# A new order of loads and of work in the opening of a transformer-like kernel, and its first constants on another queue

## The chip, the cores and the metric

One Trainium2 chip, of which one core is used. The metric is the device time of one execution in microseconds (us). The kernel before takes 1350.43 us (median of three runs, 1349.74 to 1351.45).

The core's engines run in parallel, each with its own list of instructions in order: TensorE (PE, with its weight loads as PEld), VectorE (DVE), ScalarE (ACT), GpSimd (POOL) and SyncE (SP), which here only issues loads. They wait for each other by semaphores.

## The reference

Two layers over 256 latent tokens and 256 context tokens of width 1024, in float32. The first layer mixes tokens by an mLSTM, the second by multi-head latent attention; each is followed by a gated convolutional feed-forward network. What the opening computes is the start of the first layer, for the latent tokens x with condition c and for the context with condition c_ctx:

```python
def _modulation(cond, w, b):
    m = jax.nn.silu(cond) @ w + b              # w: 1024 x 6144
    return jnp.split(m[:, None, :], 6, axis=-1)

def _modulate(x, shift, scale):
    return x * (1 + scale) + shift
...
ml = _modulation(c, ada_w[i], ada_b[i])
mc = _modulation(c_ctx[None, :], ada_w[i], ada_b[i])
hl = _modulate(x, ml[0], ml[1])
hc = _modulate(xc, mc[0], mc[1])
...
x_m = h @ w_up                                 # 1024 x 2048, inside the mLSTM mixer
```

So: two products of a single row with a matrix (shift and scale), an elementwise step, and a matrix product.

## The kernel before, in words

A float32 product is made of three products of numbers split in a high and a low part (hi, lo): hi times hi, hi times lo, lo times hi. The split is a cast by ScalarE and a subtraction by VectorE. Weights come in a stream of pieces of 128 x 1024 numbers through a class `Stream`; each piece is loaded by SyncE into one of a few buffers, split into one of three `w` buffers and used.

The opening (`start_up`) works on eight tiles f = 0 to 7, each 128 of the 1024 input channels, and multiplies them with the first six column blocks (`NUP`) of w_up. For each tile it loads from memory:

- `adaw`: the modulation's weights. For f under 4 (`NFD`) two pieces with shift and scale, 512 KB each; for f from 4 on one piece with the shift alone.
- `adat`, for f from 4 on: the scale's weights transposed, 512 KB; the scale is then not made on TensorE but by sums on VectorE.
- `xT`: the tile's tokens transposed, 256 KB.
- `raw`: the tile's rows of w_up, 384 KB.

Beside these come a few constants (`sm`, whose first 32 columns hold the conditions, and the rest, 211 KB) and the two conditions spread over all partitions (`bc`, 512 KB each).

The work on a tile is cut into steps with names, and a list, `PLAN` (lines 53 to 61), gives the order in which they are written out. Within the opening TensorE, VectorE, ScalarE and SyncE keep that order (`manual_schedule`), each for its own instructions; beyond it a planner orders most of the work by its estimates and priorities. The steps for tile f:

- `Zn`: n matmuls of zeros, 512 columns each, ahead of all else (TensorE, L710).
- `rowsf0`, `rowsf1`: condition times `adaw`, on column groups of the array (TensorE, L548). For f from 4 on there is only `rowsf0`.
- `copyf`: the result out of PSUM (VectorE for f = 0, else ScalarE, L555).
- `Tf`: small matmuls that turn the rows into columns (TensorE, L560).
- `colsf`: bias added (VectorE, L567).
- `sumf0`, `sumf1`, f from 4 on: the scale of either condition, a product with `bc` summed up (VectorE, L576). `siluj` prepares `bc` (ScalarE, L744).
- `hf0`, `hf1`: the modulation of either half of the tokens, into the high part (L664 on VectorE or L666 on ScalarE); `xxf0`, `xxf1`: the same in full precision; `hlof`: the low part (VectorE, L741).
- `whif`, `wlof`: high and low part of the tile's w_up rows (ScalarE L715, VectorE L720). There are three `w` buffers, so `whi` of tile f waits until the ups of tile f - 3 are done.
- `upf0`, `upf1`, `upf2`: hi times hi, hi times lo, lo times hi, six matmuls of 512 columns each, one per column block, added up in six PSUM banks over all tiles (TensorE, L732).

Loads are issued by SyncE in program order (`load(f)`, L684): tiles 0 to 3, then `bc`, then tile 4; the loads of tiles 5 to 7 are written behind `wlo0` to `wlo2`, since their w_up rows go into buffers that these free. Tiles 3 and 4 borrow two other buffers for them. Behind the opening `w_up` goes on with ten more column blocks from the stream (L462 to L464, three matmuls for each of eight tiles), evacuates the six held banks, and computes the later modulations on VectorE beside them (L597). The main program calls `setup`, `start_up` and `w_up` in turn.

Of the kernel before, what the change touches and what calls it, by code (L numbers as in the profile page):

```python
# [7 lines left out]
F32 = mybir.dt.float32  # L8
# [9 lines left out]
T = SEQ + CTX  # L18
# [13 lines left out]
NB, NRAW, NU, NS = 3, 3, 31, 15  # L32
# [18 lines left out]
NUP = 6  # L51
NFD = 4
PLAN = """
Z7 rows00 rows01 whi0 copy0 T0 rows10 cols0 h00 h01 wlo0 xx00 xx01 up00 hlo0 rows11 up02 copy1 whi1 T1 up01
cols1 h10 h11 xx10 xx11 wlo1 hlo1 rows20 up10 rows21 up12 copy2 whi2 T2 up11 cols2 h20 h21 xx20 xx21 wlo2 hlo2 silu0
rows30 up20 rows31 up22 copy3 whi3 T3 up21 cols3 h30 h31 xx30 xx31 wlo3 hlo3 silu1
rows40 up30 copy4 sum40 T4 up32 whi4 sum41 cols4 up31 h40 h41 xx40 xx41 wlo4 hlo4
rows50 up40 copy5 sum50 T5 up42 whi5 sum51 cols5 up41 h50 h51 xx50 xx51 wlo5 hlo5
rows60 up50 copy6 sum60 T6 up52 whi6 sum61 cols6 up51 h60 h61 xx60 xx61 wlo6 hlo6
rows70 up60 copy7 sum70 T7 up62 whi7 sum71 cols7 up61 h70 h71 xx70 xx71 wlo7 hlo7 up70 up72 up71  # L60
""".split()
# [372 lines left out]
class K:  # L434
# [63 lines left out]
    def setup(self):  # L498
        nc, p = self.nc, self.pool
        a = self.a  # L500
        self.sm = p.tile([128, a["sm"].shape[1]], F32, name="sm")
        nc.sync.dma_start(self.sm[:, :32], a["sm"][:, :32])
        b1 = self.smc("ada_b")[:, 8:16]
# [13 lines left out]
        nc.vector.memset(self.zero.bitcast(F32), 0.0)  # L517
        self.condp = p.tile([128, 8, 32], F32, tag="s2", name="condp", bufs=NS)
        nc.vector.memset(self.condp, 0.0)
# [153 lines left out]
    def start_up(self):  # L673

        nc, st = self.nc, self.st
        self.hT = []
        self.xcd = self.dr.tile([16, 128, 512], F32, name="xcd")
        self.xmd = self.dr.tile([16, 128, 512], F32, name="xmd")
        self.t2d = {(p, j): self.dr.tile([128, 1024], F32, name="t2d") for p in range(2) for j in range(4)}
        self.xA, self.x1, self.xc, self.xcr = {}, {}, [], []  # L680
        w, raws = [], []
        self.adaw, self.adap, self.adar, self.adat, self.xT = {}, {}, {}, {}, []

        def load(f):  # L684
            if f < NFD:
                for h in range(2):
                    t = self.uf("adaw")
                    nc.sync.dma_start(t, self.a["adaf"][f, h])
                    self.adaw[f, h] = t
            else:  # L690
                self.adaw[f, 0] = t = self.uf("adaw")
                nc.sync.dma_start(t, self.a["adas"][f])
                self.adat[f] = t = self.uf("adat")
                nc.sync.dma_start(t, self.a["adaT"][0, 1, f])
            for op in ("w", "x") if f == 0 else ("x", "w"):
                if op == "x":
                    x = self.s2("xT")
                    nc.sync.dma_start(x, self.a["tokT"][f])
                    self.xT.append(x)
                    continue  # L700
                tag, bufs = ("ar", 2) if f in (3, 4) else ("raw", NRAW)
                r = self.pool.tile([128, 1024], F32, tag=tag, name="raw0", bufs=bufs)
                nc.sync.dma_start(r[:, :NUP * 128], st.ws[st.ids["upf", f, 0][0], :, :NUP * 128])
                raws.append(r)
            if f == 2:
                nc.sync.dma_start(self.sm[:, 32:], self.a["sm"][:, 32:])

        def warm(n):
            for _ in range(n):
                nc.tensor.matmul(ps[-1], self.zero[:, 0:128], self.zero, start=True, stop=True)  # L710

        def w_hi(f):
            t = self.pool.tile([128, 2, CW], F32R, tag="w", name="w", bufs=NB)
            n = NUP * 128
            nc.scalar.copy(t[:, 0, :n], raws[f][:, :n])  # L715
            w.append(t)

        def w_lo(f):
            t, n = w[f], NUP * 128
            nc.vector.tensor_sub(t[:, 1, :n], raws[f][:, :n], t[:, 0, :n])  # L720
            if f < 3:
                load(f + 5)

        ps = [self.ps("up") for _ in range(NUP)]
# [10 lines left out]
        def h(f, g):  # L735
            if len(self.hT) == f:
                self.hT.append(self.u("hT"))
            self.mod_part(f, g, self.hT[f][:, 0])
# [4 lines left out]
        def silu(j):  # L743
            nc.scalar.activation(self.bc[j], self.bc[j], AF.Silu)  # L744

        ops = {"Z": warm, "rows": self.ada_rows, "copy": self.ada_copy, "T": self.ada_T, "cols": self.ada_cols,
               "sum": self.ada_sum, "silu": silu, "whi": w_hi, "wlo": w_lo,
               "h": h, "xx": lambda f, g: self.mod_part(f, g, self.xT[f]), "hlo": hlo, "up": up}
        e = mybir.EngineType
        with self.tc.manual_schedule(engines={e.PE, e.DVE, e.Activation, e.SP}):  # L750
            for f in range(4):
                load(f)
            self.bc_load(False)
            load(4)
            for t in PLAN:
                name = t.rstrip("0123456789")
                ops[name](*map(int, t[len(name):]))
            st.pump(10)
        self.ps_up = ps

    def conv(self, ps, w3, b, tmp, n):
# [1512 lines left out]
```

## Time and profile before

| | |
|---|---|
| median of three runs | 1350.43 us |
| profiled execution | 1350.77 us, of which the span of the instructions is 1348.7 us |
| TensorE busy | 1335.7 us, 99% of the span |
| VectorE, ScalarE, GpSimd busy | 1072.6, 708.2, 123.1 us |
| granted TensorE clock, mean | 0.997 |
| DMA | 292.09 MB, mean 217 GB/s |
| first matmul of the weight stream behind the opening | 56.16 us (its weight load) |

The profile gives the busy time of each engine, the chain of work that ended last, the instructions in order of time with what ended the idle time before them ("<-"), and busy times by stretch. A busy TensorE may still run below its pace, since matmuls overlap and the clock varies; the granted clock is given as a share of full speed.

### The profile page before, as it was taken

The numbers are of one execution on the slowest core, as the hardware profiler recorded it, in microseconds if no ns is written. First come the engines' busy times: TensorE is split into PE (matmuls) and PEld (weight loads), VectorE is DVE, ScalarE is ACT, GpSimd is POOL, SyncE is SP. The second block draws the span as 40 slices with busy tenths as digits, with TensorE's granted clock in tenths as the row PEclk, the third lists the DMA queues.
The fourth block names the chain that finished last, engine by engine and source line by source line (L and its number), as shares of the span: only waits on it lengthen the run. The fifth ranks groups of instructions, "written<-read, shape, count | busy, mean of one in ns | idle before, by whom it ended". The sixth has DMA issues, their size and how long they took to land.

```text
span 1348.7 us, 18734 instructions
## 1 busy us (share of the span) xinstructions
PE 1335.7 (99%) x6661; PEld 1120.0 (83%) x6661; DVE 1072.6 (80%) x1774; ACT 708.2 (53%) x1239; POOL 123.1 (9%) x216
## 2 busy tenths in 40 slices
PE   8999999999999999999999999999999999999997
PEld 5777888888888888888898888888888998988886
DVE  4798757587888696777889887778887798898884
ACT  3675434435644545374644333343458757677661
POOL 0032000011011010120002000000100011000100
PEclk8999999999999999999999999999999999999999
DMA  9689748879766364756737777775877424476860
GB/s 368 250 297 347 251 155 249 251 262 316 264 199 207 111 233 131 239 195 216 237 127 245 224 243 238 239 235 164 242 259 245 137 72 157 159 214 197 267 188 32
DMA packets 88093, 292.09 MB, mean 217 GB/s; under 512 B 11640, under 2 KB 12152, under 8 KB 88000
## 3 DMA queue, kind: packets, MB, share of 16 engines
q1 hardware_dynamic: 61840, 215.77, 48.8%
q0 software_dynamic: 17520, 57.70, 14.0%
q10 hardware_dynamic: 8640, 17.44, 3.5%
q8 instruction: 52, 0.85, 0.3%
q14 instruction: 41, 0.34, 0.1%
HBM read 260.28 MB, written 30.58 MB: 216 GB/s over the span
## 4 chain that ended last, share of the span: by engine, by line
PE 95%; DMA 2%; DVE 1%; ACT 1%; SPq 0%; issue 0%; DVEq 0%; ACTq 0%
PE fin L1589 8%; PE y L1673 7%; PE fin L462 6%; PE fin L464 6%; PE tok L462 6%; PE fin L463 6%; PE tok L463 6%; PE tok L464 6%; PE qk L462 4%; PE qk L464 4%; PE qk L463 4%; PE y L463 4%; PE y L462 4%; PE y L464 4%; PE up L462 1%; PE up L464 1%
## 5 line engine op out<-in xcount | busy, mean ns | idle before, releaser
L378 DVE TENSOR_TENSOR w<-raw,w 128x1024 fp32r<-128x1024 f32 (+1 forms) x256 | 307.8, 1206 | 112.5 <-ACT w L375 111.8
L375 ACT CAST w<-raw 128x1024 fp32r<-128x1024 f32 (+1 forms) x256 | 265.2, 1038 | 240.7 <-PE tok L464 84.4
L597 DVE SCALAR_TENSOR_TENSOR junk<-ar,bc 128x1024 f32<-128x1024 f32 x128 | 155.9, 1218 | 3.2 <-ACT mod L612 2.0
L463 PE MATMUL fin<-h,w 128*128 128x512 f32 (+1 forms) x376 | 141.2, 376 | 0.0
L462 PE MATMUL fin<-h,w 128*128 128x512 f32 (+1 forms) x376 | 141.2, 376 | 0.0
L464 PE MATMUL fin<-h,w 128*128 128x512 f32 (+1 forms) x376 | 141.1, 375 | 0.0
L1589 PE MATMUL fin<-h,w 128*128 128x256 f32 (+1 forms) x624 | 108.7, 337 | 0.0
L1589 PEld LDWEIGHTS fin<-h,w 128*128 128x128 f32 x624 | 95.9, 190 | 12.5
L462 PE MATMUL qk<-xc,w 128*128 128x512 f32 x256 | 100.4, 392 | 0.0
L464 PE MATMUL qk<-xc,w 128*128 128x512 f32 x256 | 99.7, 390 | 0.0
L463 PE MATMUL qk<-xc,w 128*128 128x512 f32 x256 | 99.6, 389 | 0.0
L463 PEld LDWEIGHTS fin<-h,w 128*128 128x128 f32 x376 | 70.8, 188 | 12.9
L464 PEld LDWEIGHTS fin<-h,w 128*128 128x128 f32 x376 | 70.8, 188 | 12.9
L462 PEld LDWEIGHTS fin<-h,w 128*128 128x128 f32 x376 | 70.7, 188 | 12.8
L464 PEld LDWEIGHTS qk<-xc,w 128*128 128x128 f32 x256 | 48.1, 188 | 10.1
L463 PEld LDWEIGHTS qk<-xc,w 128*128 128x128 f32 x256 | 48.1, 188 | 9.7
L462 PEld LDWEIGHTS qk<-xc,w 128*128 128x128 f32 x256 | 48.1, 188 | 9.7
L771 ACT ACTIVATE fg<-fg 128x512 f32<-128x512 f32 (+1 forms) x44 | 23.1, 526 | 57.3 <-DVE fg L769 51.0
L462 PE MATMUL tok<-w,hT 128*128 128x512 f32 x128 | 49.9, 390 | 0.0
L464 PE MATMUL tok<-w,hT 128*128 128x512 f32 x128 | 49.8, 389 | 0.0
L463 PE MATMUL tok<-w,hT 128*128 128x512 f32 x128 | 49.8, 389 | 0.0
L1673 PE MATMUL y<-w,fz 128*128 128x512 f32 x198 | 46.7, 393 | 0.3 <-DVE w L378 0.2
(489 smaller groups left out, 3141.2 us busy)
## 6 DMA issues: line engine op xcount, KB each, us to landing
raw<-in_ws SPq DMA_DIRECT2D x281, 512.0 KB, 4.7
ar<-in_adaT SPq DMA_DIRECT2D x80, 512.0 KB, 4.9
raw<-in_ws POOLq DMA_DIRECT2D x13, 512.0 KB, 7.2
raw<-in_ws SPq DMA_DIRECT2D x12, 384.0 KB, 6.0
adaw<-in_adaf SPq DMA_DIRECT2D x8, 512.0 KB, 6.5
xmd<-xr POOLq DMA_DIRECT2D x16, 256.0 KB, 4.8
xcd<-cv POOLq DMA_DIRECT2D x16, 256.0 KB, 4.9
xs<-xmd POOLq DMA_DIRECT2D x16, 256.0 KB, 5.5
```

What stands on the lines that cost most here:

```text
L375: k.nc.scalar.copy(h[:, :cols], src)
L378: k.nc.vector.tensor_sub(l[:, :cols], src, h[:, :cols])
L462: mm(out, w[0], x[0], start=start, stop=False)
L463: mm(out, w[0], x[1], start=False, stop=False)
L464: mm(out, w[1], x[0], start=False, stop=stop)
L597: nc.vector.scalar_tensor_tensor(o, w, 1.0, self.bc[j], op0=ALU.mult, op1=ALU.mult, accum_out=col[:, k, j:j + 1])
L771: nc.scalar.activation(tmp[:, :n], tmp[:, :n], AF.Silu)
L1589: nc.tensor.matmul(ps[:, :m], w[x][:, k * 128:(k + 1) * 128], hT(k)[:, :m], start=k == 0 and x == j, stop=k == 7 and x != j, skip_group_ch ...
L1673: nc.tensor.matmul(ps[b], a[:, p, ts], w[q][:, cs], start=j == 0 and n == 0 and not more, stop=j == end and n == 2, skip_group_check=True)
```

## The change

Five things change.

1. The order of the steps (`PLAN`) is another one. up00 stands ahead of rows10; rows of two or three tiles stand together; the sums of a tile come earlier against its h; the last four steps remain up61, up70, up72, up71.
2. New steps `Yn`: n matmuls of zeros with 256 columns, one behind rows00, two behind rows01, four behind T0.
3. The loads have a list of their own, `LOADS`, cut where a load of w_up rows would need a buffer that is not free yet. In it a40 comes ahead of a31, w3 and x3, the `bc` loads come behind x3, and t4, a50 and later loads are mixed anew. The bytes are the same.
4. The first 32 columns of `sm` are loaded by ScalarE's queue instead of SyncE's.
5. `condp`, the padded condition, lives in a buffer of the large ring (31 buffers) instead of the small one (15).

Lists become dictionaries where tiles are now touched out of order. The diff, with its last part cut to what matters:

```diff
@@ -51,13 +51,15 @@
 NUP = 6
 NFD = 4
 PLAN = """
-Z7 rows00 rows01 whi0 copy0 T0 rows10 cols0 h00 h01 wlo0 xx00 xx01 up00 hlo0 rows11 up02 copy1 whi1 T1 up01
-cols1 h10 h11 xx10 xx11 wlo1 hlo1 rows20 up10 rows21 up12 copy2 whi2 T2 up11 cols2 h20 h21 xx20 xx21 wlo2 hlo2 silu0
-rows30 up20 rows31 up22 copy3 whi3 T3 up21 cols3 h30 h31 xx30 xx31 wlo3 hlo3 silu1
-rows40 up30 copy4 sum40 T4 up32 whi4 sum41 cols4 up31 h40 h41 xx40 xx41 wlo4 hlo4
-rows50 up40 copy5 sum50 T5 up42 whi5 sum51 cols5 up41 h50 h51 xx50 xx51 wlo5 hlo5
-rows60 up50 copy6 sum60 T6 up52 whi6 sum61 cols6 up51 h60 h61 xx60 xx61 wlo6 hlo6
-rows70 up60 copy7 sum70 T7 up62 whi7 sum71 cols7 up61 h70 h71 xx70 xx71 wlo7 hlo7 up70 up72 up71
+Z7 rows00 Y1 rows01 whi0 copy0 Y2 T0 cols0 h00 h01 wlo0 xx00 xx01 Y4 hlo0 up00 rows10 rows11 up02 copy1 T1 up01 whi1
+rows20 wlo1 cols1 h10 rows21 xx10 h11 up12 xx11 hlo1 copy2 up11 whi2 up10 T2 cols2 rows30 h21 xx21 rows31 rows40 copy3
+h20 xx20 wlo2 up20 hlo2 T3 cols3 h30 copy4 whi3 h31 T4 xx30 xx31 wlo3 hlo3 silu0 silu1 whi4 up21 sum40 up22 sum41 up30
+cols4 up31 wlo4 h41 h40 xx41 sum50 rows50 xx40 hlo4 copy5 whi5 up32 up42 up40 T5 sum51 cols5 rows60 h50 wlo5 up41 h51
+copy6 xx51 xx50 up52 sum60 T6 rows70 sum61 whi6 cols6 copy7 hlo5 up50 wlo6 T7 h60 h61 sum70 xx60 xx61 up51 cols7 sum71
+hlo6 whi7 wlo7 h71 h70 xx71 xx70 up60 hlo7 up62 up61 up70 up72 up71
+""".split()
+LOADS = """
+a00 a01 w0 x0 a10 a11 x1 w1 a20 a21 x2 w2 sm a30 a40 a31 w3 x3 bc0 bc1 t4 a50 w4 x4 t5 x5 w5 a60 t6 w6 a70 x6 t7 w7 x7
 """.split()
 
 TAIL = {"mout": 4, "aout": 7, "fout1": 6}
@@ -499,7 +501,7 @@
         nc, p = self.nc, self.pool
         a = self.a
         self.sm = p.tile([128, a["sm"].shape[1]], F32, name="sm")
-        nc.sync.dma_start(self.sm[:, :32], a["sm"][:, :32])
+        nc.scalar.dma_start(self.sm[:, :32], a["sm"][:, :32])
         b1 = self.smc("ada_b")[:, 8:16]
         nc.vector.tensor_scalar(b1, b1, 1.0, None, op0=ALU.add)
         jp = p.tile([128, 128], I32, tag="s2", name="jp", bufs=NS)
@@ -515,7 +517,7 @@
         nc.vector.memset(self.k1, 1.0)
         self.zero = p.tile([128, 512], F32R, tag="s2", name="zero", bufs=NS)
         nc.vector.memset(self.zero.bitcast(F32), 0.0)
-        self.condp = p.tile([128, 8, 32], F32, tag="s2", name="condp", bufs=NS)
+        self.condp = self.uf("condp")[:, 0:256].rearrange("p (k n) -> p k n", n=32)
         nc.vector.memset(self.condp, 0.0)
         self.keps = p.tile([128, 1], F32, name="keps")
         nc.vector.memset(self.keps, EPS)
@@ -673,47 +675,56 @@
     def start_up(self):
 
         nc, st = self.nc, self.st
-        self.hT = []
+        self.hT = {}
         self.xcd = self.dr.tile([16, 128, 512], F32, name="xcd")
         self.xmd = self.dr.tile([16, 128, 512], F32, name="xmd")
         self.t2d = {(p, j): self.dr.tile([128, 1024], F32, name="t2d") for p in range(2) for j in range(4)}
         self.xA, self.x1, self.xc, self.xcr = {}, {}, [], []
-        w, raws = [], []
+        w = {}
         self.adaw, self.adap, self.adar, self.adat, self.xT = {}, {}, {}, {}, []
 
-        def load(f):
-            if f < NFD:
-                for h in range(2):
-                    t = self.uf("adaw")
-                    nc.sync.dma_start(t, self.a["adaf"][f, h])
-                    self.adaw[f, h] = t
-            else:
-                self.adaw[f, 0] = t = self.uf("adaw")
-                nc.sync.dma_start(t, self.a["adas"][f])
-                self.adat[f] = t = self.uf("adat")
-                nc.sync.dma_start(t, self.a["adaT"][0, 1, f])
-            for op in ("w", "x") if f == 0 else ("x", "w"):
-                if op == "x":
-                    x = self.s2("xT")
-                    nc.sync.dma_start(x, self.a["tokT"][f])
-                    self.xT.append(x)
-                    continue
-                tag, bufs = ("ar", 2) if f in (3, 4) else ("raw", NRAW)
-                r = self.pool.tile([128, 1024], F32, tag=tag, name="raw0", bufs=bufs)
-                nc.sync.dma_start(r[:, :NUP * 128], st.ws[st.ids["upf", f, 0][0], :, :NUP * 128])
-                raws.append(r)
-            if f == 2:
-                nc.sync.dma_start(self.sm[:, 32:], self.a["sm"][:, 32:])
+        loads = list(LOADS)
+        raws, self.xT, self.bc = {}, {}, [None, None]
+
+        def load(last):
+            while loads:
+                if loads[0][0] == "w" and int(loads[0][1]) > last:
+                    return
+                t = loads.pop(0)
+                op, *n = t.rstrip("0123456789"), *map(int, t[len(t.rstrip("0123456789")):])
+                f = n[0] if n else 0
+                if op == "a":
+                    self.adaw[f, n[1]] = t = self.uf("adaw")
+                    nc.sync.dma_start(t, self.a["adaf"][f, n[1]] if f < NFD else self.a["adas"][f])
+                elif op == "t":
+                    self.adat[f] = t = self.uf("adat")
+                    nc.sync.dma_start(t, self.a["adaT"][0, 1, f])
+                elif op == "x":
+                    self.xT[f] = t = self.s2("xT")
+                    nc.sync.dma_start(t, self.a["tokT"][f])
+                elif op == "bc":
+                    self.bc[f] = t = self.pool.tile([128, 1024], F32, tag="acc", name="bc", bufs=2)
+                    nc.sync.dma_start(t, self.a["crow"][f:f + 1, :].to_broadcast([128, 1024]))
+                elif op == "sm":
+                    nc.sync.dma_start(self.sm[:, 32:], self.a["sm"][:, 32:])
+                else:
+                    tag, bufs = ("ar", 2) if f in (3, 4) else ("raw", NRAW)
+                    raws[f] = t = self.pool.tile([128, 1024], F32, tag=tag, name="raw0", bufs=bufs)
+                    nc.sync.dma_start(t[:, :NUP * 128], st.ws[st.ids["upf", f, 0][0], :, :NUP * 128])
 
         def warm(n):
             for _ in range(n):
                 nc.tensor.matmul(ps[-1], self.zero[:, 0:128], self.zero, start=True, stop=True)
+
+        def warm2(n):
+            for _ in range(n):
+                nc.tensor.matmul(ps[-1][:, 0:256], self.zero[:, 0:128], self.zero[:, 0:256], start=True, stop=True)
 
         def w_hi(f):
             t = self.pool.tile([128, 2, CW], F32R, tag="w", name="w", bufs=NB)
             n = NUP * 128
             nc.scalar.copy(t[:, 0, :n], raws[f][:, :n])
-            w.append(t)
+            w[f] = t
 
         def w_lo(f):
             t, n = w[f], NUP * 128
...
-            if len(self.hT) == f:
-                self.hT.append(self.u("hT"))
+            if f not in self.hT:
+                self.hT[f] = self.u("hT")
...
-        ops = {"Z": warm, "rows": self.ada_rows, ...
+        ops = {"Z": warm, "Y": warm2, "rows": self.ada_rows, ...
...
-            for f in range(4):
-                load(f)
-            self.bc_load(False)
             load(4)
             for t in PLAN:
                 name = t.rstrip("0123456789")
                 ops[name](*map(int, t[len(name):]))
             st.pump(10)
         self.ps_up = ps
+        self.hT = [self.hT[f] for f in range(8)]
```

More of the change, by code (lines that the diff above doesn't have):

```diff
@@ L744, in silu @@
             nc.scalar.activation(self.bc[j], self.bc[j], AF.Silu)
-        ops = {"Z": warm, "rows": self.ada_rows, "copy": self.ada_copy, "T": self.ada_T, "cols": self.ada_cols,
+        ops = {"Z": warm, "Y": warm2, "rows": self.ada_rows, "copy": self.ada_copy, "T": self.ada_T, "cols": self.ada_cols,
                "sum": self.ada_sum, "silu": silu, "whi": w_hi, "wlo": w_lo,
```

## The prediction

> **What bounds the kernel now.** I read the page first, for the whole, and then the busy times by stretch, to see whether a shorter opening can reach the end.
>
> ```profile
> span 1348.7 us, 18734 instructions
> ...
> PE 1335.7 (99%) x6661; PEld 1120.0 (83%) x6661; DVE 1072.6 (80%) x1774; ACT 708.2 (53%) x1239; POOL 123.1 (9%) x216
> ...
> PE 95%; DMA 2%; DVE 1%; ACT 1%; SPq 0%; issue 0%; DVEq 0%; ACTq 0%
> ```
> ```profile
> 0.00:56.16 56.16, 50.79 (x303) 0.94 0.86 327
> 56.16:100.00 43.84, 43.84 (x200) 1.00 0.81 277
> ...
> 1000.00:1340.00 340.00, 339.50 (x2015) 1.00 0.52 166
> ```
> The second fence has TensorE alone: stretch, length, busy time (instructions), granted clock, share of the DMA engines, GB/s. TensorE is busy without a hole from 56.16, where the first matmul of the weight stream follows the opening, almost to the end. So microseconds taken from the opening should come off the span one for one, and only the opening (5.4 us idle, clock 0.94) has some to give. I then went through it in order of time. Its start (start, duration, engine, line, what; PEld is the weight load that opens a step on TensorE):
>
> ```profile
> 0.74 1.28 ACT L523 ACT_TABLE_LOAD   x1 [0.74 <-PEq L2264]
> 0.74 0.38 SPq L502 DMA_DIRECT2D sm<-in_sm  x1
> 1.18 0.89 SPq L688 DMA_DIRECT2D adaw<-in_adaf  x2
> 1.49 3.35 PE L710 MATMUL up<-zero 128*128 128x512 f32 x7 [1.49 <-DVE zero L517]
> 2.65 0.18 DVE L524 COPY condp<-cond 128x16 f32<-128x16 f32 x1
> 5.12 0.19 PEld L548 LDWEIGHTS adar<-adaw,condp 128*32 128x32 f32 x8 [1.00 <-issue]
> 6.34 0.16 PEld L548 LDWEIGHTS adar<-adaw,condp 128*32 128x32 f32 x8 [1.03 <-DMA adaw<-in_adaf]
> 7.53 0.61 PE L560 MATMUL adar<-sums,adarow 128*128 128x2 f32 x4 [0.55 <-DVE adarow L555]
> 8.43 0.60 ACT L666 ACTIVATE hT<-xT,mod 128x256 fp32r<-128x256 f32 x1
> 9.62 0.20 PEld L548 LDWEIGHTS adar<-adaw,condp 128*32 128x32 f32 x8 [1.58 <-DMA adaw<-in_adaf]
> 10.63 2.21 PEld L732 LDWEIGHTS up<-hT,w 128*128 128x128 f32 x6 [0.81 <-issue]
> 13.49 0.20 PEld L548 LDWEIGHTS adar<-adaw,condp 128*32 128x32 f32 x8 [0.65 <-issue]
> 14.50 1.49 PEld L732 LDWEIGHTS up<-hT,w 128*128 128x128 f32 x6 [0.81 <-issue]
> 16.04 0.64 PEld L560 LDWEIGHTS adar<-sums,adarow 128*128 128x128 f32 x4
> ```
> The steps are rows00 (5.12), rows01 (6.34), T0 (7.53), rows10 (9.62), up00 (10.63), rows11 (13.49), up02 (14.50), T1 (16.04). h01 ends at 9.03, so up00 had its operands 1.6 us before it ran: it stood behind rows10, which waited for its load. Next, one cycle of the steady part: rows20, rows21, up12, T2, up11, rows30.
>
> ```profile
> 18.19 0.16 PEld L548 LDWEIGHTS adar<-adaw,condp 128*32 128x32 f32 x8 [0.36 <-issue]
> 20.34 0.16 PEld L548 LDWEIGHTS adar<-adaw,condp 128*32 128x32 f32 x8 [0.36 <-issue]
> 20.91 1.23 PEld L732 LDWEIGHTS up<-hT,w 128*128 128x128 f32 x6 [0.41 <-issue]
> 22.18 0.64 PEld L560 LDWEIGHTS adar<-sums,adarow 128*128 128x128 f32 x4
> 22.74 1.22 PEld L732 LDWEIGHTS up<-hT,w 128*128 128x128 f32 x6
> 24.31 0.16 PEld L548 LDWEIGHTS adar<-adaw,condp 128*32 128x32 f32 x8 [0.35 <-issue]
> ```
> Here TensorE waits for no data: it is its own list that lasts 6.12 us a tile. And the end of the opening:
>
> ```profile
> 32.66 2.59 PEld L732 LDWEIGHTS up<-hT,w 128*128 128x128 f32 x12
> 35.60 0.38 PEld L548 LDWEIGHTS adar<-adaw,condp 128*32 128x32 f32 x16 [0.35 <-issue]
> ...
> 42.71 1.22 DVE L576 SCALAR_TENSOR_TENSOR junk<-adat,bc 128x1024 f32<-128x1024 f32 x1
> 45.50 1.09 ACT L666 ACTIVATE hT<-xT,mod 128x256 fp32r<-128x256 f32 x2 [2.55 <-DVE mod L567]
> 45.90 0.38 PEld L548 LDWEIGHTS adar<-adaw,condp 128*32 128x32 f32 x16 [0.35 <-issue]
> 46.65 1.23 PEld L732 LDWEIGHTS up<-hT,w 128*128 128x128 f32 x6 [0.38 <-ACT hT L666]
> ...
> 48.26 2.61 PEld L732 LDWEIGHTS up<-hT,w 128*128 128x128 f32 x12
> ...
> 52.16 3.95 PEld L732 LDWEIGHTS up<-hT,w 128*128 128x128 f32 x18 [1.29 <-ACT hT L666]
> 53.13 0.69 DVE L741 TENSOR_TENSOR hT<-xT,hT 128x512 fp32r<-128x512 f32 x1 [1.28 <-ACT xT L666]
> ```
> Now it is late data: the two sums of a tile run on VectorE right before that tile's h, and ScalarE waits 2.55 us a tile for them, until TensorE waits too.
>
> **Unit costs on TensorE.** From start to start, at full clock: an up before T takes 1.27 (20.91 to 22.18); an up before rows 1.57 (22.74 to 24.31); two ups before rows 2.94 (32.66 to 35.60). So an up is 1.36 to 1.37, rows behind an up cost 0.21 more, T behind an up 0.09 less. Rows take 0.57 (20.34 to 20.91), T of an early tile 0.56 (22.18 to 22.74), T of a late one 0.34 (47.92 to 48.26, from the same rows: 46.65 plus 1.27). A check on the old list, from rows20 at 18.19 to where up70 would follow: 18 ups 24.5, 8 rows 4.6, T 2.5, 7 switches to rows 1.5, 6 from up to T -0.5, in all 32.6, so 50.8. 48.26 plus two ups (2.72) is 51.0. The units hold to 0.2.
>
> **The change, part by part.**
> *First constants.* Their issue (0.38) leaves SyncE's queue, so every load there starts 1.18 - 0.74 = 0.44 earlier. On ScalarE it stands beside the table load, which ends at 2.02. If it is issued only behind that, condp is ready some 1.3 later than 2.83, at 4.1; rows00 cannot start before the warm-up ends at 4.84. Covered, cost 0 either way. rows01 waits for its load, so all from there to h01 comes 0.44 earlier: h01 ends at 8.59.
> *up00 ahead of rows10.* up00 at 8.59 instead of 10.63: -2.04. rows10, done before it until now, follows at 0.57.
> *Extra warm-up matmuls* (1, 2 and 4 of 256 columns). The seven old ones, of 512 columns, took 3.35, so one of 256 takes at most 0.24: at most 0.24, 0.48 and 0.96, in gaps of 0.55 (before rows01), 0.55 (before T0) and 9.03 - 8.14 = 0.89 (behind T0). At worst 0.1 sticks out; taken as 0. What they may bring is the clock:
>
> ```profile
> 4.87:8.28 3.41, 1.88 (x20) 1.00 1.01 370
> 8.28:11.67 3.39, 2.05 (x11) 0.50 1.03 409
> 11.67:15.07 3.40, 3.40 (x14) 0.50 1.02 408
> ```
> The clock fell to 0.50 at 8.28, behind a stretch 55% busy (1.88 of 3.41), stayed there over one 60% busy and rose at 15.07 behind one wholly busy. This cost up00 13.49 - 10.63 - 1.57 = 1.29, rows11 1.01 - 0.57 = 0.44, up02 1.54 - 1.27 = 0.27: 2.0. In the new list the stretch to 8.28 holds 1.88 plus seven short matmuls (at the full clock's pace, a sixth of 1.36 halved, 0.11 each: 0.8), some 2.7 of 3.41 or 78%. The trace has no stretch between 60% and 100%, so the gain lies between 0 and 2.0, with a middle: a low clock only to 11.67, since the next stretch is full from 8.59, costs (11.67 - 8.59)/2 = 1.5. I take the full clock, by a small margin: short holes (at most 0.6 each) look more like the full stretch than like the 1.5 ahead of 9.62.
> The Trainium skill, "TensorE: Matmul & The Clock Gate", Part 1, says that a monitor halves the clock behind an idle window of about 3.4 us and restores it behind a busy one, and that these windows run free of the kernel's start. The distances here (3.41, 3.39, 3.40) agree; that the windows would lie elsewhere in other runs, so that the new matmuls help in some and not in others, speaks against the change, and one profile cannot show it.
> *Fewer switches.* Before, rows follow an up nine times; after, three times (rows10, 20, 50), and T three times (rows30, 60, 70). No row shows rows behind T: bounds 0 (it is a mere switch of step) and 0.21 (as behind an up). I take 0.21, since the hole of 0.36 before the weight load belongs to rows. Gain 6 to 3 times 0.21, 0.6 taken, 1.3 at best.
> *Sums and h apart.* sum40 to sum71 now come a step or more before they are wanted, and the end loses its waits: 46.65 for 46.47 (45.90 + 0.57), and 52.16 for 51.0: 1.3.
> *The loads' order.* Loads run at about 408 GB/s:
>
> ```profile
> 20.00:25.00 5.00, 5.00 (x35) 3.06 (x34) 1.91 (x5) 2.86 (x5) 0.00 (x0) 1.00 1.03 408
> ```
> (the last number; before it the busy times of five engines, clock and DMA share). Behind a01 (5.90), a31 is preceded by 5.85 MB with itself: 14.3 us, so 20.2, or 20.6 with the 0.4 that a10 (9.62) was late by the same rule. TensorE wants it (rows31) at 8.59 + 6.1 (to rows20) + 5.7 (to T2's end) + 0.8 = 21.2. Margin 0.6 to 1.0, the tightest of the list. t4 lands near 26.1; two sums (2.5) and h4 (1.1), with a pass of 0.7 ahead of them on VectorE and one of 0.8 on ScalarE, bring h4 to 31.2, wanted by up42 at about 32.4. The last load, x7, with 13.85 MB behind a01, lands at about 39.8, wanted near 47. So the loads cost 0, and eat what they are late beyond 0.6. The first weights of the stream behind: three 512 KB loads and its own follow x7, 5.1 us, so 45; ScalarE and VectorE passes to 47.5, before the opening's new end. condp in another ring and dicts for lists add no work on a path.
>
> **The sum.** Along the new list from up00 at 8.59: 24 ups 32.6; 10 rows 5.7; T1 to T3 1.7; T4 to T7 1.4; six switches to rows 1.3; six from up to T -0.5. That is 42.2, so the opening ends at 50.8 instead of 56.16: -5.4. By parts: -2.0 + 0.6 (rows10 later) - 2.0 - 0.6 - 1.3 = -5.3, the same. The profiled execution took 1350.77 (span 1348.7 and 2.07 around it), 0.34 above the median of 1350.43, so on the median: 1350.4 - 5.4 = **1345.0**.
>
> **The rivals.**
> *The clock still falls.* For it: 78% is nearer to 60% than to 100%. Against: no hole is longer than 0.6 us. One half-clock stretch to 11.67 leaves 5.4 - 1.5 = 3.9: 1346.5. Down to 15.07 it is 3.2, leaving 2.2: 1348.2.
> *The loads become the bound.* For it: SyncE issues in order, and the margin at rows31 is under 1 us. Against: the rows with 408 and 409 GB/s, in three stretches. At 350 GB/s a31 comes 2.4 later, so some 1.8 of the 5.4 is lost: 1346.8.
> *Nothing arrives.* The stage behind takes the gain back, since VectorE and not TensorE sets its pace:
>
> ```profile
> 65.00:70.00 5.00, 5.00 (x24) 4.14 (x23) 5.00 (x10) 4.14 (x9) 1.61 (x3) 1.00 0.59 188
> ```
> VectorE (third of the busy times) is full there. Against: its last pass of the opening, hlo7 (53.13 to 53.82), is wanted by up71 at 49.4, so it must end at least 4.4 earlier too. Time 1349.5 to 1350.5.
> *Slower.* The order behind the opening on VectorE is the planner's; if it puts the sums of the later modulation (1.22 each, by the row at 42.71) ahead of the evacuations of the six held PSUM banks, TensorE waits for a bank at its third tile. Each pass in the way costs at most 1.22, so five in the way undo the gain and seven make 1353. No such wait stands in the profile now.
>
> **How the numbers follow.** Full clock, loads in time: 0.47, 1345.0, own range 1344.0 (rows behind T free) to 1346.0. Clock low to 11.67, or loads a little late: 0.26, 1346.5. Low to 15.07 or both: 0.13, 1348.2. Nothing arrives: 0.08. Slower: 0.06. Range 1343.9 to 1348.4, which holds the first three. What can be told from no change is 0.2%, 2.7 us, so faster means under 1347.7: the first two and about half of the third, 0.79; same 0.15; slower 0.06.
>
> **What would show it.** Right: up00 at about 8.6; up steps of 1.36 from there with a clock of 1.00; rows20 near 14.7, rows31 near 21.2 with no wait for adaw; no ScalarE wait for sums before the last up; the stream's first matmul near 50.8 and TensorE whole behind it. Wrong: a clock of 0.50 behind 8.28, TensorE released by adaw or adat loads, new waits on PSUM banks behind 51 us, or the shift at 50.8 not found again at 1340.

## The result, and the profile after

The changed kernel takes 1370.85 us (median of six runs, 1369.84 to 1371.50), beside 1349.95 for the kernel before (six runs, 1349.43 to 1351.45). The ratio is 1.0152, with a 95% interval of 1.0139 to 1.0165: it is slower by 20.9 us. The forecast was 1345.0. Its profiled execution took 1369.84.

The page of the kernel after: span, busy times of the engines, the chain that ended last.

```profile
span 1368.1 us, 18747 instructions
...
PE 1358.1 (99%) x6668; PEld 1120.5 (82%) x6668; DVE 1073.7 (78%) x1774; ACT 709.6 (52%) x1239; POOL 123.0 (9%) x216
...
PE 99%; DMA 0%; DVE 0%; SPq 0%; issue 0%; DVEq 0%
```

TensorE is busy for 22.4 us more with seven matmuls more, all of 256 columns of zeros. The other engines have as many instructions as they had, and are busy for as long within 1.4 us. Where those 22 us lie is seen in the opening's end. The kernel after in order of time (start, duration, engine, line, what), and then the stream's first matmul in the kernel before:

```profile
42.80 10.04 PE L743 MATMUL up<-hT,w 128*128 128x512 f32 x42
52.68 0.40 PE L464 MATMUL up<-hT,w 128*128 128x512 f32 x1
52.92 0.39 PE L465 MATMUL up<-hT,w 128*128 128x512 f32 x1
```
```profile
56.38 0.39 PE L462 MATMUL up<-hT,w 128*128 128x512 f32 x1
```

The stream's first matmul stands at 52.68 instead of 56.38 (56.16 in the table before is its weight load), so the opening did become 3.7 us shorter. From there to the end of the span it is 1315.4 us (1368.1 less 52.68), where it was 1292.3 (1348.7 less 56.38): 23.1 us came in behind the opening, where no line of code was changed. Two stretches of 100 us there, first of the kernel after, then of the one before. The columns are the stretch, its length, busy time and count of PE, PEld, DVE, ACT and POOL, granted clock, share of the DMA engines, GB/s:

```profile
200.00:300.00 100.00, 100.00 (x430) 80.50 (x429) 71.91 (x71) 41.25 (x44) 7.88 (x12) 1.00 0.76 245
800.00:900.00 100.00, 100.00 (x430) 80.34 (x429) 75.93 (x119) 37.88 (x67) 5.85 (x9) 1.00 0.70 227
```
```profile
200.00:300.00 100.00, 100.00 (x443) 82.80 (x442) 73.68 (x72) 42.41 (x45) 7.88 (x12) 1.00 0.80 254
800.00:900.00 100.00, 100.00 (x443) 82.78 (x442) 77.68 (x120) 38.62 (x70) 5.70 (x9) 1.00 0.73 235
```

This is the main reading of the case. TensorE is busy without a hole in all four rows and the clock is 1.00 in all four, but it gets through 430 matmuls in the time in which it got through 443: 232.6 ns each instead of 225.7. There is no wait to be found, because there is none. The share of busy time (99% in both) cannot show it; the count beside it does. Added up over the whole trace, the distances from start to start of the matmuls with 512 columns (4,999 in either kernel) come to 1169.5 us after and 1146.0 before: +23.5. Those with 256 columns come to 133.6 and 135.4: seven more of them took 1.8 us less.

The start of the opening, kernel after:

```profile
0.74 0.39 SPq L622 DMA_DIRECT2D ar<-in_adaT  x1
0.74 0.41 ACTq L504 DMA_DIRECT2D sm<-in_sm  x1
1.19 0.90 SPq L698 DMA_DIRECT2D adaw<-in_adaf  x2
...
4.55 0.22 ACT L525 ACTIVATE cond<-sm 128x16 f32<-128x16 f32 x1 [2.09 <-DMA sm<-in_sm]
5.79 0.64 PE L550 MATMUL adar<-adaw,condp 128*32 128x256 f32 x8 [0.95 <-DMA adaw<-in_adaf]
9.69 2.76 PE L743 MATMUL up<-hT,w 128*128 128x512 f32 x6
```
```profile
5.30:8.70 3.40, 2.53 (x24) 1.00 1.03 413
8.70:12.10 3.40, 3.40 (x11) 0.50 1.03 405
12.10:15.50 3.40, 3.40 (x29) 1.00 1.03 405
```

Three things differ from the forecast. A 512 KB load for the later modulation (ar, L622) now stands first in SyncE's list, ahead of a00, so the loads of the opening start at 1.19, no earlier than before, and rows00 waits for its weights until 5.79. The 16 KB of first constants, which were there at about 2.4 us, are there at 4.55. And the clock (second fence, TensorE alone) fell to 0.50 for one stretch, 8.70 to 12.10, behind one that was 74% busy (2.53 of 3.40), so up00 took 2.76.

### The profile page after: what moved, and what is told of

Read it like the earlier page. It is cut to its first block, busy times and chain, and to the rows that moved or that the text cites. A ratio compares the mean times of both kernels' runs of the same rounds, so it can differ in the third digit from the quotient of the medians.

```text
span 1368.1 us, 18747 instructions
## 1 busy us (share of the span) xinstructions
PE 1358.1 (99%) x6668; PEld 1120.5 (82%) x6668; DVE 1073.7 (78%) x1774; ACT 709.6 (52%) x1239; POOL 123.0 (9%) x216
## 4 chain that ended last, share of the span: by engine, by line
PE 99%; DMA 0%; DVE 0%; SPq 0%; issue 0%; DVEq 0%
PE fin L1598 8%; PE y L1682 8%; PE fin L464 6%; PE tok L464 6%; PE fin L465 6%; PE tok L466 6%; PE fin L466 6%; PE tok L465 6%; PE qk L466 4%; PE qk L464 4%; PE qk L465 4%; PE y L465 4%; PE y L466 4%; PE y L464 4%; PE up L743 3%; PE up L464 1%
## 5 line engine op out<-in xcount | busy, mean ns | idle before, releaser
L465 PE MATMUL fin<-h,w 128*128 128x512 f32 (+1 forms) x376 | 143.0, 380 | 0.0
L464 PE MATMUL fin<-h,w 128*128 128x512 f32 (+1 forms) x376 | 143.0, 381 | 0.0
L466 PE MATMUL fin<-h,w 128*128 128x512 f32 (+1 forms) x376 | 142.9, 380 | 0.0
L464 PE MATMUL qk<-xc,w 128*128 128x512 f32 x256 | 101.8, 398 | 0.0
L466 PE MATMUL qk<-xc,w 128*128 128x512 f32 x256 | 101.1, 395 | 0.0
L465 PE MATMUL qk<-xc,w 128*128 128x512 f32 x256 | 101.1, 395 | 0.0
L466 PEld LDWEIGHTS fin<-h,w 128*128 128x128 f32 x376 | 70.5, 187 | 15.1
L465 PEld LDWEIGHTS fin<-h,w 128*128 128x128 f32 x376 | 70.5, 187 | 15.1
L780 ACT ACTIVATE fg<-fg 128x512 f32<-128x512 f32 (+1 forms) x44 | 23.1, 526 | 56.2 <-DVE fg L778 49.9
```

The lines of the kernel that those rows point to most:

```text
L464: mm(out, w[0], x[0], start=start, stop=False)
L465: mm(out, w[0], x[1], start=False, stop=False)
L466: mm(out, w[1], x[0], start=False, stop=stop)
L780: nc.scalar.activation(tmp[:, :n], tmp[:, :n], AF.Silu)
```

## The experiments

What could make each matmul slower without a wait? The program as built gives the places of the buffers in on-chip memory (bytes from the start of a partition). The large ring of 31 buffers (tag u) holds h, and with it most moving operands or weights; the ring w holds the split weights of the stream.

```
kernel                        ring u   ring w   distance w - u, modulo 256
before                         39104   194752     0
after                          38368   194752   224
before, condp line alone       38368   194752   224
after, keps ahead of condp     38400   194752   192
after, 32 bytes ahead of w     38368   194784     0
after, condp in small ring     39104   194752     0
```

Buffers are laid out in the order of first use. With condp in it, the large ring is first used in `setup`, ahead of keps (4 bytes, padded to 32) and the other small constants, and so moves down by 736 bytes, which is 224 modulo 256. My theory was that the pace depends on the distance of the two operands modulo some small power of two, first taken as 64 (A in the expectations). The rivals: the absolute place of a ring (A2), and the new order or the early load.

**One line in the kernel before.**

```diff
-        self.condp = p.tile([128, 8, 32], F32, tag="s2", name="condp", bufs=NS)
+        self.condp = self.uf("condp")[:, 0:256].rearrange("p (k n) -> p k n", n=32)
```

> The kernel before with one line of the change alone: condp is taken from the large ring. Order of work and loads as before; the large ring moves from byte 39104 to 38368. Theory A: 4,370 matmuls of 512 columns at 6.6 ns more and some 510 of 256 columns at 3 ns less make 23 to 27 us: 1373 to 1377, pace 233 ns in the stages with weights from the ring w. Rival B: 1350, no change.

Measured: 1374.87 us (1374.05 to 1375.63), ratio 1.0180 (1.0165 to 1.0195). This one line costs 24.4 us; nothing else of the change is needed. It brings the early load too, here behind the first constants:

```profile
0.74 0.38 SPq L502 DMA_DIRECT2D sm<-in_sm  x1
1.18 0.42 SPq L620 DMA_DIRECT2D ar<-in_adaT  x1
1.65 0.90 SPq L688 DMA_DIRECT2D adaw<-in_adaf  x2
...
6.41 0.64 PE L548 MATMUL adar<-adaw,condp 128*32 128x256 f32 x8 [1.57 <-DMA adaw<-in_adaf]
```

rows00 starts 1.3 us later than in the kernel before. The early load hangs on the condp line, then, and not on SyncE's emptier queue. Why the planner puts it there wasn't examined.

**keps ahead of condp**, in the changed kernel: two lines change places, and the ring moves by 32 bytes.

```diff
-        self.condp = self.uf("condp")[:, 0:256].rearrange("p (k n) -> p k n", n=32)
-        nc.vector.memset(self.condp, 0.0)
         self.keps = p.tile([128, 1], F32, name="keps")
         nc.vector.memset(self.keps, EPS)
+        self.condp = self.uf("condp")[:, 0:256].rearrange("p (k n) -> p k n", n=32)
+        nc.vector.memset(self.condp, 0.0)
```

> The changed kernel with two lines swapped: the 4-byte constant keps is allocated ahead of condp. No engine's work changes but the order of two small memsets; in the program as built, the large ring (31 buffers, tag u) starts at byte 38400 of a partition instead of 38368, so that it lies at the same place within 64 bytes as the ring of split weights (tag w, at 194752). Theory A (the changed kernel is slow because a matmul of 512 columns takes 233 instead of 227 ns when its two operands lie at different places within 64 bytes): pace 227 ns everywhere, the opening ends near 51.7 us instead of 52.7, the time is 1345.5 to 1347, that is 4 below before. Rival B (the new order of work and loads is what costs, somewhere behind the opening): still 1369 to 1371.

Measured: 1360.14 us (1358.95 to 1360.85), ratio 1.0070 (1.0054 to 1.0087). About half of the loss is gone, where theory A wanted all of it gone. The same two stretches tell why:

```profile
200.00:300.00 100.00, 100.00 (x430) 80.60 (x429) 71.92 (x71) 41.15 (x44) 7.88 (x12) 1.00 0.79 246
800.00:900.00 100.00, 100.00 (x439) 82.05 (x438) 80.17 (x128) 38.20 (x68) 6.41 (x10) 1.00 0.73 237
```

In the first, where w is the moving operand (the products tok), the pace is still 430 in 100 us; in the second, where u moves against weights in w, it is 439. So the direction matters, and 64 is not the period: theory A falls in this form. The matmul classes show 228.9 ns with u moving, 233.3 with w moving. A larger period with several paces was left.

**32 bytes ahead of the ring w**, in the changed kernel.

```diff
+            if f == 0:
+                nc.gpsimd.memset(self.pool.tile([128, 8], F32, name="pad"), 0.0)
             t = self.pool.tile([128, 2, CW], F32R, tag="w", name="w", bufs=NB)
```

> The changed kernel with a tile of 32 bytes allocated (and cleared by GpSimd) ahead of the ring w, which so moves from byte 194752 to 194784; the large ring stays at 38368. Both rings are now 32 bytes off a multiple of 64. Theory A (the places of the two operands relative to each other decide): pace 227 ns, 1345.5 to 1347. Rival A2 (a moving operand that doesn't start on a multiple of 64 bytes takes one line of 64 bytes more, 33 instead of 32, which is 3%): now both kinds of stage have such a moving operand, pace 233 ns, 1369 or more.

Measured: 1347.34 us (1345.00 to 1348.96), ratio 0.9975 (0.9965 to 0.9984).

```profile
200.00:300.00 100.00, 100.00 (x443) 82.80 (x442) 72.53 (x69) 41.83 (x43) 8.78 (x13) 1.00 0.80 256
800.00:900.00 100.00, 100.00 (x443) 82.81 (x442) 77.68 (x120) 36.83 (x66) 5.31 (x9) 1.00 0.72 230
```

443 again, and 1142.9 us for all 512-column matmuls. The ring u still lies where it lies in the slow kernel, and neither ring lies where it does in the kernel before; only their distance is a multiple of 256 again. The absolute place (A2) falls, and so do the new order and the early load as causes of the loss.

**The pace by itself.** A kernel that only runs matmuls, 60 in a row, with the places of moving operand (mv) and weights (st) shifted between the rows. The work of the reference is left out.

```diff
+                for i in range(N):
+                    k = s + 128 * (i % 4)
+                    nc.tensor.matmul(ps[:, :n], st[:, k:k + 128], mv[:, m:m + n], start=i == 0, stop=i == N - 1)
```

> None of the reference's work: only matmuls in a row, 60 each of 33 kinds, all with new weights each time, on data from one weight array; the output is not computed. The kinds differ in columns (512, 384, 256, 128), in where the moving operand starts (0, 16, 32, 64 or 96 bytes off a multiple of 64) and in where the weights start (0 to 288 bytes off). Theory A: at 512 columns 227 ns where both starts agree within 64 bytes and 233 where they are 32 apart; at 256 columns 120 and 117. Rival A2: 227 where the moving operand starts on a multiple of 64 bytes, 233 where it doesn't, whatever the weights. Open: what 4, 8 or 16 bytes do, and whether the period is 64 bytes.

A part of its timeline (start, and duration of 60, the last one's end modelled; the pace below is the mean distance from start to start from the fifth matmul of a row to its last). In the first four rows the weights lie 0, 48, 64 and 256 bytes further on in the partition than the moving operand, modulo 256; in the last one both are moved on by 32:

```profile
21.92 13.77 PE L45 MATMUL qaa<-mv,st 128*128 128x512 f32 x60
...
91.30 14.16 PE L45 MATMUL qaf<-mv,st 128*128 128x512 f32 x60
105.30 14.15 PE L45 MATMUL qag<-mv,st 128*128 128x512 f32 x60
...
161.28 13.82 PE L45 MATMUL qak<-mv,st 128*128 128x512 f32 x60
...
216.69 13.81 PE L45 MATMUL qao<-mv,st 128*128 128x512 f32 x60
```

That is 226.7, 233.3, 233.3, 227.1 and 227.0 ns a matmul. Shifting both by 32 leaves the pace, shifting one by less than 256 slows it. (Both at 16 took 231.1, so places that are no multiple of 32 have a price of their own; the program lays out every buffer at multiples of 32.) Matmuls of 384 columns took 173.3 ns with the weights 0 and 32 further on, those of 128 columns 111.7 at either: no effect at these two.

**The map over the period**, the same kernel with the moving operand at every 32 bytes up to 512, and with bfloat16.

> None of the reference's work: matmuls in a row, 60 of a kind, new weights each time; the output is not computed. The weights start at a fixed place, the moving operand 0 to 512 bytes behind it in steps of 32 (float32r, 512 columns) or 0 to 256 (256 columns), and 0 to 256 bytes in bfloat16. Theory A' (the distance modulo 256 bytes decides): at 512 columns 226.7 ns at 0, 256 and 512, 229 at 64 and 320, 233 elsewhere; at 256 columns 120 at 0 and 256, 113 at 192, 117 to 118 elsewhere. If the period is 128 or 512 instead, 128 or 256 shows it. No theory says what bfloat16 does.

Here the moving operand is moved instead; "ahead" means that it lies further on than the weights. (The weights 64 further on, as above, are a moving operand 192 ahead.) 512 columns with the moving operand 0, 32, 64 and 256 bytes ahead, 256 columns with it 0 and 192 ahead, and one row of bfloat16 (192 ahead):

```profile
22.61 13.76 PE L51 MATMUL qaa<-mv,st 128*128 128x512 f32 x60
36.20 14.17 PE L51 MATMUL qab<-mv,st 128*128 128x512 f32 x60
50.21 13.91 PE L51 MATMUL qac<-mv,st 128*128 128x512 f32 x60
...
134.01 13.79 PE L51 MATMUL qai<-mv,st 128*128 128x512 f32 x60
...
259.07 7.36 PE L51 MATMUL qar<-mv,st 128*128 128x256 f32 x60
...
301.76 7.00 PE L51 MATMUL qax<-mv,st 128*128 128x256 f32 x60
...
374.68 13.11 PE L51 MATMUL qbe<-mb,sbf 128*128 128x512 bf16 x59
```

| moving ahead by, modulo 256 | 0 | 32 | 64 | 96 | 128 | 160 | 192 | 224 |
|---|---|---|---|---|---|---|---|---|
| ns, 512 columns | 226.7 | 233.3 | 228.9 | 233.4 | 233.4 | 234.3 | 233.3 | 233.3 |
| ns, 256 columns | 120.0 | 117.8 | 117.8 | 119.9 | 118.7 | 117.3 | 113.4 | 118.4 |

From 256 to 512 the row of 512 columns repeats within 0.1 ns: the period is 256 bytes. It explains every kernel so far. In the changed one a moving u is 32 ahead, a moving w 224: 233.3 both ways. With keps first it is 64 and 192: 228.9 and 233.3, as measured in it. The last nanosecond is not settled: two rows of the kernel before this one differ from the map at the same distance (232.4 for 512 columns at 128, 116.7 for 256 columns at 32). bfloat16 took 216 ns at each of the five distances tried, 0, 32, 64, 128 and 192 (the rows start 12.95 us apart).

**condp back in the small ring**, the rest of the change left as it is.

```diff
-        self.condp = self.uf("condp")[:, 0:256].rearrange("p (k n) -> p k n", n=32)
+        self.condp = p.tile([128, 8, 32], F32, tag="s2", name="condp", bufs=NS)
```

> The changed kernel with one line undone: condp stands in the small ring again. In the program as built the large ring is back at byte 39104, 0 off the ring w modulo 256, and SyncE's list begins with the opening's own loads: the 512 KB load for the later modulation, which stands first in the changed kernel, is back behind them. Theory (this one line cost both the pace and the head start): pace 227 ns, first adaw load issued at 0.74 us, rows00 near 4.8, opening's end 50.5 to 52.5 us by where the half-clock stretch falls, time 1344 to 1347. Rival (the load came first because SyncE's queue was empty without the first constants): the load stands first all the same, rows00 near 5.8, 1346.5 to 1348.

Measured: 1345.64 us (1344.13 to 1347.90), ratio 0.9970 (0.9958 to 0.9982). This is within 0.7 us of the time that had been forecast for the whole change; but the kernel before took 1349.74 beside it, so the gain is 4.1 us, where 5.4 had been forecast.

```profile
0.74 0.87 SPq L698 DMA_DIRECT2D adaw<-in_adaf  x2
...
5.07 0.18 DVE L526 COPY condp<-cond 128x16 f32<-128x16 f32 x1
...
5.30 0.91 PE L550 MATMUL adar<-adaw,condp 128*32 128x256 f32 x8 [0.45 <-DVE condp L526]
9.13 1.65 PE L743 MATMUL up<-hT,w 128*128 128x512 f32 x6 [0.31 <-ACT hT L668]
15.15 1.07 PE L550 MATMUL adar<-adaw,condp 128*32 128x256 f32 x16
21.87 1.08 PE L550 MATMUL adar<-adaw,condp 128*32 128x256 f32 x24 [0.43 <-DMA adaw<-in_adaf]
51.42 0.39 PE L464 MATMUL up<-hT,w 128*128 128x512 f32 x1
```

The early load is gone. The stream's first matmul is at 51.42, and from there to the end of the span it is 1292.8 us (1344.2 less 51.42), beside 1292.3 before: now the gain of the opening does arrive, but for half a microsecond. rows00 waits for condp, that is for the first constants, and not for its weights.

This kernel and the changed one differ by the one line, so they also give its price without the gain of the opening. The matmuls with 512 columns come to 1142.6 us here, 26.9 less than the 1169.5 of the changed kernel, and those with 256 columns to 135.6, 2.0 more: 24.9 in all, beside a difference of 25.2 in time (1370.85 less 1345.64). By the addresses in the programs as built, 2,466 matmuls with 512 columns have a moving u 32 ahead in the changed kernel and 1,959 a moving w 224 ahead; here all of these have a distance of 0. By the map, 4,425 times 6.6 ns make 29.2 us; the 2.3 between this and 26.9 are not explained.

**First constants back on SyncE's queue** too: one more line undone.

```diff
-        nc.scalar.dma_start(self.sm[:, :32], a["sm"][:, :32])
+        nc.sync.dma_start(self.sm[:, :32], a["sm"][:, :32])
```

> As condp_s2 (the changed kernel with condp in the small ring), and with the first constants loaded by SyncE's queue as before the change. On ScalarE's queue their 16 KB landed at 4.8 us, beside the big loads, and rows00 waited for condp until 5.30. On SyncE's they should land near 2.4, and rows00 then waits for adaw, whose issue is back at 1.18: rows00 at 4.9 to 5.1. If moving the constants gains nothing: the same as condp_s2 within 0.7 us, 1345 to 1346. If it gained 0.4 as forecast: 0.4 slower, 1346.

Measured: 1345.46 us (1344.48 to 1347.20), ratio 0.9972 (0.9962 to 0.9982): the same.

```profile
0.74 0.39 SPq L504 DMA_DIRECT2D sm<-in_sm  x1
1.19 0.89 SPq L698 DMA_DIRECT2D adaw<-in_adaf  x2
...
2.91 0.18 DVE L526 COPY condp<-cond 128x16 f32<-128x16 f32 x1
4.91 0.97 PE L550 MATMUL adar<-adaw,condp 128*32 128x256 f32 x8
```

With its own place at the head of SyncE's queue the small load is used at 2.66 and rows00 starts at 4.91, right behind the warm-up; on ScalarE's queue it lands beside the large ones 2.2 us later, and rows00 starts at 5.30. The move of this load frees 0.45 us in SyncE's queue and loses 0.4 at rows00. With the load on SyncE's queue up00 starts at 8.81 instead of 9.13, but rows31 then waits 0.92 us for its weights instead of 0.43, and the stream's first matmul is at 51.60 instead of 51.42. In the time the move gains nothing.

**The early load held back, and the Y matmuls.** Three kernels with the distance mended by the 32 bytes. In `hold`, the loads for the later modulation are ordered behind the opening's last load; the second leaves out Y1, Y2 and Y4 as well; the third has `hold` with the old order of the loads under the new order of the work.

```diff
+            with self.tc.issue_after(self.last_load.ins):
+                self.nc.sync.dma_start(w, self.a["adaT"][l, c, k])
...
-Z7 rows00 Y1 rows01 whi0 copy0 Y2 T0 cols0 h00 h01 wlo0 xx00 xx01 Y4 hlo0 up00 rows10 rows11 up02 copy1 T1 up01 whi1
+Z7 rows00 rows01 whi0 copy0 T0 cols0 h00 h01 wlo0 xx00 xx01 hlo0 up00 rows10 rows11 up02 copy1 T1 up01 whi1
...
-a00 a01 w0 x0 a10 a11 x1 w1 a20 a21 x2 w2 sm a30 a40 a31 w3 x3 bc0 bc1 t4 a50 w4 x4 t5 x5 w5 a60 t6 w6 a70 x6 t7 w7 x7
+a00 a01 w0 x0 a10 a11 x1 w1 a20 a21 x2 w2 sm a30 a31 x3 w3 bc0 bc1 a40 t4 x4 w4 a50 t5 x5 w5 a60 t6 x6 w6 a70 t7 x7 w7
```

> The changed kernel with 32 bytes ahead of the ring w (pace 227 ns) and with the loads for the later modulation put behind the opening's last load in SyncE's list, by an ordering alone. condp stays in the large ring. Against the same without the ordering (1347.3): rows00 a microsecond earlier, 5.98 to about 4.8. If the early load was what made the opening late: 1345.5 to 1346.5. If the head start is swallowed by another wait: 1347.3 as without.

> As hold, without the seven short warm-up matmuls Y1, Y2 and Y4. If they keep the clock up, the half-clock stretch is longer without them and the time 1 to 2 us above hold; if the stretch is set by where the 3.4 us windows happen to lie and these matmuls are too few, the same as hold within 0.7.

> As hold, with the opening's loads in the old order (tile by tile, x3, w3 and both bc ahead of a40) under the new order of work. By 408 GB/s a40 then lands near 24.7 us, and rows40, which the new list places at about 22, holds up all behind it: 2 to 3 us above hold. If the order of loads is of no account: as hold.

Measured: `hold` 1345.47 us (1344.30 to 1346.48), ratio 0.9969 (0.9956 to 0.9981). Without the Y matmuls 1346.03 (1344.75 to 1346.69), ratio 0.9972 (0.9962 to 0.9983). With the old loads 1350.92 (1347.67 to 1353.27), ratio 1.0010 (1.0001 to 1.0019).

*The early load.* rows00 starts at 5.31 in `hold` (4.8 had been expected, but it waits for condp), 5.98 with the pad alone (1347.34 us). By the rows the early load costs some 0.5 to 0.7 us at the start. The times differ by 1.9, but they come from two chips, and the intervals of the two ratios overlap; more than the 0.7 is not shown. Differences of this size in the opening can't be followed to the end: the stream's first matmul is at 53.06 in `hold` and at 51.42 with condp in the small ring, 1.6 apart, and the spans are 1344.4 and 1344.2.

*The Y matmuls.* Their effect on the time can't be told from nothing here. What the two traces show is two courses of the clock: with them, in `hold`, rows00 took 1.08 us and the first six ups 2.93, where six take 1.66 from 14.28 on, so TensorE ran at half pace from the start to 13.39 (the profile's clock column has 1.00 there, which does not fit these durations); without them, rows00 and rows01 took 1.38 together, and only the stretch from 9.36 to 12.78 has a clock of 0.50. Of these two, the one without Y starts its first ups earlier (8.70 against 10.36).

*The old order of the loads* under the new order of the work:

```profile
20.45 1.07 PE L550 MATMUL adar<-adaw,condp 128*32 128x256 f32 x16
26.01 1.08 PE L550 MATMUL adar<-adaw,condp 128*32 128x128 f32 x16 [4.49 <-DMA adaw<-in_adas]
```
```profile
21.56:24.97 3.41, 0.00 (x0) 1.00 1.04 414
24.97:28.38 3.41, 2.37 (x19) 0.50 1.04 404
28.38:31.79 3.41, 3.41 (x12) 0.50 1.03 402
31.79:35.21 3.42, 3.42 (x9) 0.50 1.03 403
```

rows40 waits 4.49 us for its weights, and behind the empty stretch the clock is at 0.50 for three more. Both together take all that the opening gained. So the new loads are needed by the new order, and a stall here costs more than its own length: 5.4 us where 2 to 3 had been expected. The eleven executions lie 5.6 us apart, the longest with the lowest mean clock (1353.27 with 0.994, 1347.67 with 0.999).

## Why the prediction was wrong

**The step that failed** is the last sentence on the parts: "condp in another ring and dicts for lists add no work on a path". It adds no work, but it moves the large ring by 736 bytes, and with that it slows 4,425 of the 4,999 matmuls with 512 columns (before, 52 had their operands apart). They take 23.5 us more than before, and 26.9 more than with that line undone, four to five times all that the change was to bring. The unit that the sum rests on, 1.36 us for six matmuls, was taken as fixed; it is one of this layout, and 1.40 (six times 233.3 ns) in the other. None of the rivals had it: the one on the slower side named VectorE's order and the PSUM banks, of which no wait is seen in the kernel after. And the step stood at a cost of 0 with no bound on the other side. Of the signs given for a wrong prediction, three came. Two are in the opening, the clock of 0.50 from 8.70 and rows00 released by its load at 5.79, and are part of why it gained 3.7 us and not 5.4. The one that points at the cause is "the shift at 50.8 not found again at 1340": the 3.7 us gained at 52.68 were a loss of 19.4 at the end of the span.

**What held, without that line** (forecast, then measured in the kernel with condp in the small ring):

- The time: 1345.0, and 1345.64. This is in part luck: the gain was 4.1 us (1349.74 less 1345.64) and not 5.4.
- From up00 to the stream's first matmul: 42.2, and 42.3 (9.13 to 51.42). Ups, T and the switches between them came to 36.5, as in the sum; the ten rows took 5.4 instead of 5.7, and a wait of 0.43 that stood at 0 made up for it.
- rows20 6.1 behind up00, and 6.0 (9.13 to 15.15).
- The sums cost no wait any more: behind 24 us TensorE's ups wait for nothing.
- "microseconds taken from the opening should come off the span one for one": the stream's first matmul came 5.0 us earlier (56.38 to 51.42), and the span is 4.5 shorter.

**What was off by less:**

- up00 at 8.59: it came at 9.13. condp "ready ... at 4.1" was a bound from ScalarE's side alone, from when its queue is free. What is late is the transfer: condp was ready at 5.25 (5.07 and 0.18), so rows00 waited. "Covered, cost 0 either way" cost 0.4 us, as much as the move freed.
- "Margin 0.6 to 1.0" for the loads at rows31: there was none; TensorE waited 0.43 for adaw until 21.87. That load was put at 20.2 to 20.6, and it came over a microsecond later. It is the tightest place, as was said, and the old order of loads shows what lies behind it.
- "I take the full clock": it held in this kernel (the stretch from 5.90 to 9.31 was 88% busy, 2.99 of 3.41, and the clock stayed) but not in the changed kernel (74% busy, and it fell to 0.50 until 12.10, the middle case of the range), and not in `hold`. One trace of each kernel does not show how often either happens; the mean clocks of the executions (0.996 to 0.998 in the changed kernel) would fit a course that differs from one to the next. The Trainium skill, "TensorE: Matmul & The Clock Gate", Part 1, says that the windows of the clock's monitor run free of the kernel's start. The traces agree: in stretches of 3.41 us, full pace came back at 12.10 in the changed kernel, at 13.39 in `hold`, at 15.1 in the kernel before, and the first matmul starts at 1.49 in all three.

## What to carry to other kernels

A line that only moves a buffer can change the pace of most matmuls of a kernel; so compare where the buffers lie before and after an edit, as you compare the instructions. When TensorE is fully busy in both profiles and the time still differs, count its instructions in equal stretches at equal clock: 443 against 430 in 100 us is a cause that no list of waits shows. A 32-byte pad, or a line put elsewhere, mends it; and the rest of a change should be judged with the layout held fixed.

## What the runs showed of the hardware

- The pace of float32r matmuls (fp32r in the rows, the type of the split numbers) depends on the distance of the moving operand from the weights within a partition, modulo 256 bytes: 226.7 ns at 0, 228.9 with the moving operand 64 ahead, 233.3 to 234.3 at the other multiples of 32 (232.4 in one row at 128), for 512 columns at a granted clock of 1.00. For 256 columns the best place is another one (113.4 ns at 192, 120.0 at 0); 384 and 128 columns showed no difference between weights 0 and 32 further on. That the next weights are read while the operand streams, and that both then meet in the same part of the memory, would fit, but is only argued.
- bfloat16 took 216 ns for 512 columns at each of the five distances tried. The Trainium skill, "TensorE: Matmul & The Clock Gate", section "Wait — 56ns, not 53.3ns?", gives the distance from start to start by the columns alone, 215.7 ns for 512. The bfloat16 rows agree; for float32r the measurement differs by 11 to 19 ns, and here it decides.
- A 16 KB load issued on ScalarE's queue at the same moment as 512 KB loads on SyncE's was used 4.1 us after its issue began (0.74 to 4.82), and 1.9 us after (0.74 to 2.66) when it went ahead of them on theirs.
- By the map, the stages with 256 columns could gain some 6 ns a matmul from a moving operand 192 ahead. That is an estimate and was not tried in the kernel, where the two rings serve both kinds.
